# A linear-attention gate product stacked for one pass, and its chunk-end decays issued one step earlier

## The chip, the cores and the metric

The kernel runs on one core of a Trainium2 chip. The metric is the device time of one execution in microseconds (us), as the median of several runs. TensorE (PE in the profile, PEld for its weight loads) multiplies, VectorE (DVE), ScalarE (ACT) and GpSimd (POOL) do the elementwise work, and SyncE (SP) issues most DMAs.

## The reference, cut to what matters

Two layers of a streaming encoder over 512 tokens of width 1024. Each layer has a token mixer with three groups of heads (retention, stick-breaking attention, gated linear attention) and a convolutional feed-forward part. The change lies in the gated linear attention. `glr` is a projection of rank 16 and `b_i` the running sum of the log decays within a chunk of 64 tokens:

```
log_alpha = log_sigmoid(glr @ gla_w2 + gla_b) / 16        # (512 x 16) @ (16 x 256)
bcum  = cumsum(log_alpha within a chunk)
blast = bcum at the chunk's end
kv    = einsum(k * exp(blast - bcum), v)                  # decays to the chunk's end
inter = (q * exp(bcum)) @ state                           # decays from the chunk's start
state = exp(blast) * state + kv
w     = exp(-|b_t - b_s|)                                 # inside a chunk, either direction
intra = (q k w summed over d) @ v
```

All of it is in f32 and has to hold f32 accuracy.

## The kernel before, in words

Large products take three passes each: both operands are split into a rounded part (`hi`, type fp32r) and the rest (`lo`), and `mm3` sums hi·hi, hi·lo and lo·hi. For weights, `unit` loads 512 KB into `raw` (L360), ACT casts it to `hi` (L361) and DVE subtracts to get `lo` (L362). Activations `hnh`, `hnl` are split once. A projection `proj_T` is 24 matmuls of 128x512 into one PSUM bank named `pj`; everything else goes into banks named `ps`.

A mixer runs four kinds of work as generators, and a string of letters (`TOK`) sets in which turn they are advanced: `p` one projection, `g` a step of linear attention, `s` a step of stick-breaking or retention, `f` four loads of the modulation weights (`ada`, 256 KB each), which DVE multiplies and sums (L255) while the mixer runs. `ada` tiles have three buffers, `raw` two. A scheduling layer then puts every engine's instructions into one fixed order, by its own estimates; at run time an engine executes that order strictly, so an instruction that waits holds all behind it on its engine.

`gla_pair` (L653) handles two heads. It makes the gate (a product with K of 16 in plain f32: `w2` 16x256 and `glrT` 16x512, tiles filled at L569 to L574), the running sum `b` by a scan (L665), and then seven score steps `n` = 0 to 6. Step `n` issues 16 small score products, then, for `n` < 6, the decays of the next level (`decays`, L669 to L679), then merges the scores under a mask (L701). Behind the last step (`n` = 6) stand `kd` (L706, exponential on ACT at L226, L709), `qd` (an exponential and L711) and `dl`. The next step of the generator transposes `kd` on PE (L95), copies the result (L722) and multiplies it with the values; DVE rolls the states forward (L740, L742), and the output products follow.

There are two such pairs in each layer, so four gate products and four `kd` chains in the program. Each gate product issues from the two lines

```
with seq("g"):
    PE.matmul(ps, res["w2"][:, j * P : j * P + P], res["glrT"], start=True, stop=True)
```

Of the kernel before, what the change touches and what calls it, by code (L numbers as in the profile page):

```python
# [12 lines left out]
F32R = mybir.dt.float32r  # L13
# [3 lines left out]
ALU = mybir.AluOpType  # L17
AX = mybir.AxisListType

P = 128  # L20
S = 512
# [40 lines left out]
LEVELS = (64, 32, 16, 8, 4, 2)  # L62
# [36 lines left out]
def trunk(ctx: ExitStack, tc: tile.TileContext, A, out, dbg=None):  # L99
# [18 lines left out]
    def nm(s):  # L118
        cnt[0] += 1
        return f"{s}_{cnt[0]}"  # L120

    def T(tag="m", shape=(P, 512), dt=F32):
        tag = TMAP.get(tag, tag)
        return tiles[tag].tile(list(shape), dt, tag=tag, name=nm(tag + "_"))

    def small(n):
        return sp.tile([P, 8], F32, tag="s", name=nm("s"))[:, :n]

    def bank(t):
        t = PMAP[t]  # L130
        return banks[t].tile([P, 512], F32, tag=t, name=nm(t))
# [4 lines left out]
    def psz():  # L136
        return bank("pz")
# [4 lines left out]
    def psg():  # L142
        return bank("pg")

    V, SC, G, PE = nc.vector, nc.scalar, nc.gpsimd, Recorder(nc.tensor)

    @contextmanager
    def seq(kind):

        mode = MODE[kind]  # L150
        m = (None, PE.last, PE.lastp)[mode]
        if m is not None:
            with tc.issue_after(m.ins):
                yield
        else:
            yield
        if kind == "p":
            PE.lastp = PE.last
# [4 lines left out]
    def ld(t, src, gated=False, kind=None):  # L163
        q = QUEUE.get(kind, "sp")
        if q != "sp":
            return (G if q == "g" else SC).dma_start(t, src)


        m = lastw[0] if gated else start["ld"]
        if m is None:  # L170
            r = nc.sync.dma_start(t, src)
        else:
            with tc.issue_after(m.ins):
                r = nc.sync.dma_start(t, src)
        if start["on"]:
            start["ld"] = r
        return r
# [5 lines left out]
    def as32(t):  # L183
        return t.bitcast(F32)
# [39 lines left out]
    def act(*a, **k):  # L224
        with tc.issue_after(tables[0].ins):
            last_act[0] = SC.activation(*a, **k)  # L226
# [316 lines left out]
    def mixer(l, hnh, hnl, after):  # L543
# [3 lines left out]
        res = {}  # L547
# [16 lines left out]
        def use_gv(tb, ps):  # L564
            vtok[tb] = T("gv", (P, 272))
            SC.copy(vtok[tb], ps[:, 0:272])
            if tb == NTB - 1:
                w2 = T("gl", (16, 256))
                ld(w2, A["gla_w2"][l], True)  # L569
                ps = psg()  # L570
                for t in range(NTB):
                    PE.transpose(ps[0:16, t * P : t * P + P], vtok[t][:, 256:272], ident)
                glrT = T("gl", (16, S))
                SC.copy(glrT, ps[0:16, :])  # L574
                res["w2"], res["glrT"] = w2, glrT

        trig, dms = [], {}

# [14 lines left out]
        def project(n):  # L593
            if n[:2] in ("sv", "gv", "rv"):
                src, w, use = {"sv": (A["wsv"], 384, use_sv), "gv": (A["wgv"], 272, use_gv),
                               "rv": (A["wrv"], 384, use_rv)}[n]
                if n in start:
                    for tb, ps in enumerate(start.pop(n)):
                        use(tb, ps)
                else:  # L600
                    yield from proj_tok(src[l], w, hnh, hnl, use)
                res[n] = True
                return
            res[n] = project_T(n[:2], int(n[2]))
            yield
# [47 lines left out]
        def gla_pair(j):  # L653
            gq, gk, _ = need(f"gq{j}", f"gk{j}", "gv")
            ps = psg()
# [13 lines left out]
            def decays(m):  # L669
                E = T("ge")  # L670
                bv = b.rearrange("p (n h t) -> p n h t", h=2, t=m // 2)
                Ev = E.rearrange("p (n h t) -> p n h t", h=2, t=m // 2)
                r = bv[:, :, 0, m // 2 - 1 : m // 2].to_broadcast([P, S // m, m // 2])
                V.tensor_tensor(Ev[:, :, 0, :], r, bv[:, :, 0, :], ALU.subtract)
                V.tensor_tensor(Ev[:, :, 1, :], bv[:, :, 1, :], r, ALU.subtract)
                act(E, E, AF.Exp, scale=-1.0 / TAU)
                kt, qt = T("ge"), T("ge")
                V.tensor_tensor(kt, gk, E, ALU.mult)
                V.tensor_tensor(qt, gq, E, ALU.mult)  # L679
                return kt, qt  # L680
# [3 lines left out]
            for n in range(len(LEVELS) + 1):  # L684
                kt, qt = cur

                ps = [psg(), (psz, pso, psg)[GB]()]
                with seq("g"):
                    for c in range(NCH):
                        odd, cs = 64 * (c % 2), slice(c * CH, c * CH + CH)  # L690
                        for h in range(2):
                            PE.matmul(ps[h][odd : odd + 64, c // 2 * CH : c // 2 * CH + CH], kt[64 * h : 64 * h + 64, cs],
                                      qt[64 * h : 64 * h + 64, cs], start=True, stop=True)
                if n < len(LEVELS):
                    cur = decays(LEVELS[n])
                for h in range(2):
                    p3 = ps[h][:, 0 : S // 2].rearrange("p (c t) -> p c t", t=CH)
                    if n == 0:
                        SC.copy(sc[:, h], p3)
                    else:  # L700
                        V.copy_predicated(sc[:, h],  # L701
                                          C["lev"][:, n - 1, :].unsqueeze(1).to_broadcast([P, NCH // 2, CH]), p3)
                if n == len(LEVELS):
                    b3 = b.rearrange("p (c t) -> p c t", t=CH)
                    kd, qd = T("gl"), T("gl")
                    V.tensor_tensor(kd.rearrange("p (c t) -> p c t", t=CH),  # L706
                                    b3[:, :, CH - 1 : CH].to_broadcast([P, NCH, CH]), b3, ALU.subtract)
                    act(kd, kd, AF.Exp, scale=-1.0 / TAU)
                    V.tensor_tensor(kd, kd, gk, ALU.mult)  # L709
                    act(qd, b, AF.Exp, scale=-1.0 / TAU)  # L710
                    V.tensor_tensor(qd, qd, gq, ALU.mult)  # L711
                    dl = small(NCH)
                    act(dl, b3[:, :, CH - 1], AF.Exp, scale=-1.0 / TAU)
                yield
            tap(f"gs{l}{j}", sc.rearrange("p h c t -> p (h c t)"))

            ps = psg()
# [100 lines left out]
        def ret_pair(j):  # L818
# [12 lines left out]
            with seq("r"):  # L831
# [4 lines left out]
            yield from normed(ro[j], pvl[:, PV["rn"] + j : PV["rn"] + j + 1])  # L836

        chains = {"g": chain(*(gla_pair(j) for j in range(2))),
                  "s": chain(*((sb_pair if x[0] == "s" else ret_pair)(int(x[1])) for x in SORD.split()))}
        alive = set(chains)  # L840
# [50 lines left out]
        for tb in range(NTB):  # L891
            cs = slice(tb * P, tb * P + P)
            ps = psz()
# [79 lines left out]
    if WARM:  # L973

        ps = psz()
# [196 lines left out]
```

## Time and profile before

| | us |
|---|---|
| median of 3 runs | 1393.89 |
| the runs | 1394.96, 1389.60, 1393.89 |
| the profiled execution | 1389.99 |
| its span, first to last instruction | 1388.2 |
| PE busy | 1352.6 (97%) |
| DVE busy | 837.9 (60%) |
| ACT busy | 633.9 (46%) |

The two mixers lie at about 15 to 345 us and 700 to 1015 us of the span, the feed-forward parts behind each. A busy PE is not a PE at its peak, since its matmuls overlap and their ends are modelled: the distance from one matmul's start to the next says more than its duration. "Idle before" is the time an engine had nothing running, with the instruction that ended the wait. An engine's granted clock of 1.00 is 2.4 GHz and 0.50 is 1.2 GHz.

### The profile page before, as it was taken

Reading aid. Unit: us, or ns where it says so; the run is one execution under the profiler, and the core shown is the slowest. Engines: PE = TensorE matmul, PEld = TensorE weight load, DVE = VectorE, ACT = ScalarE, POOL = GpSimd, SP = SyncE. Lnnn points to the kernel's source line nnn. Section 1 sums busy time; section 2 is a strip of 40 time slices with the busy share of each in tenths; the row PEclk is TensorE's granted clock in tenths of the full one; section 3 lists DMA queues with packets and bytes.
Section 4 is the critical chain, followed back from the end, with each engine's and each line's share of the span. In section 5 each row is a group of like instructions: output and inputs, shape, how many; then the busy total and the mean of one; then the engine's idle time right before and its main releaser. Section 6 shows DMA issues by size and latency. Waiting matters only on the chain.

```text
span 1388.2 us, 19780 instructions
## 1 busy us (share of the span) xinstructions
PE 1352.6 (97%) x7619; PEld 1109.0 (80%) x7619; DVE 837.9 (60%) x1572; ACT 633.9 (46%) x1033; POOL 66.5 (5%) x121
## 2 busy tenths in 40 slices
PE   8999999999999999999999999999999999999997
PEld 5887667767988878888899877777898888888886
DVE  4559997666888864524563587777575444443232
ACT  5456465755533333322254556665564333332220
POOL 1000000001000000000030000000110000000000
PEclk9999999999999999999999999999999999999999
DMA  9635461215677852233753222111433222222233
GB/s 323 223 120 168 157 220 50 77 33 178 229 251 253 265 184 95 91 106 116 245 172 123 69 92 76 39 69 61 146 128 121 91 96 102 91 102 96 91 106 106
DMA packets 72463, 186.23 MB, mean 134 GB/s; under 512 B 8832, under 2 KB 9904, under 8 KB 72368
## 3 DMA queue, kind: packets, MB, share of 16 engines
q1 hardware_dynamic: 69056, 176.39, 37.6%
q0 software_dynamic: 3008, 8.41, 1.7%
q8 instruction: 60, 0.98, 0.3%
q14 instruction: 35, 0.29, 0.1%
q10 hardware_dynamic: 304, 0.16, 0.0%
HBM read 176.51 MB, written 8.41 MB: 133 GB/s over the span
## 4 chain that ended last, share of the span: by engine, by line
PE 63%; DVE 16%; DMA 9%; issue 6%; ACT 4%; POOL 1%; SPq 0%; DVEq 0%; POOLq 0%; ACTq 0%
PE pj L92 36%; PE ps L92 27%; DMA ada<-ada 8%; DVE lo L362 3%; DVE ada L255 3%; ACT hi L361 1%; DMA raw<-wsv 0%; POOL s L295 0%; DMA m__117_557<-ada 0%; DMA raw<-wu 0%; ACT junk L307 0%; DVE m__180_958 L701 0%; DMA raw<-wT 0%; DMA m__6_119<-x 0%; DVE hnl L342 0%
## 5 line engine op out<-in xcount | busy, mean ns | idle before, releaser
L362 DVE TENSOR_TENSOR lo<-raw,hi 128x1024 fp32r<-128x1024 f32 (+2 forms) x208 | 245.8, 1183 | 260.0 <-ACT hi L361 251.6
L92 PE MATMUL pj<-hnh,hi 128*128 128x512 f32 x976 | 384.0, 393 | 0.8 <-DVE mod1sc L260 0.8
L92 PE MATMUL pj<-hnh,lo 128*128 128x512 f32 x976 | 382.3, 392 | 2.2 <-DVE lo L362 2.2
L92 PE MATMUL pj<-hnl,hi 128*128 128x512 f32 x976 | 382.1, 392 | 0.0
L361 ACT CAST hi<-raw 128x1024 fp32r<-128x1024 f32 (+2 forms) x208 | 211.4, 1018 | 334.0 <-PE pj L92 174.5
L92 PEld LDWEIGHTS pj<-hnh,lo 128*128 128x128 f32 x976 | 183.7, 188 | 40.6 <-DVE lo L362 2.5
L92 PEld LDWEIGHTS pj<-hnh,hi 128*128 128x128 f32 x976 | 183.7, 188 | 40.7 <-issue 3.6
L92 PEld LDWEIGHTS pj<-hnl,hi 128*128 128x128 f32 x976 | 183.8, 188 | 37.5 <-issue 0.8
L255 DVE SCALAR_TENSOR_TENSOR ada<-ada,cB 128x512 f32<-128x512 f32 x160 | 106.7, 686 | 32.2 <-DMA ada<-ada 31.8
L295 POOL TENSOR_TENSOR s<-s,nhalf 128x1 f32<-128x1 f32 x32 | 19.3, 604 | 728.0 <-DVE s L293 720.1
L92 PE MATMUL pj<-hi,hnh 128*128 128x384 f32 (+1 forms) x160 | 51.2, 320 | 0.0
L92 PE MATMUL pj<-hi,hnl 128*128 128x384 f32 (+1 forms) x160 | 51.0, 319 | 0.0
L92 PE MATMUL pj<-lo,hnh 128*128 128x384 f32 (+1 forms) x160 | 51.0, 319 | 0.0
L92 PE MATMUL ps<-hnh,hi 128*128 128x256 f32 x128 | 36.6, 287 | 2.6 <-ACT hnh L341 2.6
L92 PE MATMUL ps<-hnl,hi 128*128 128x256 f32 x128 | 36.6, 286 | 1.2 <-DVE hnl L342 1.2
L92 PE MATMUL ps<-hnh,lo 128*128 128x256 f32 x128 | 36.1, 283 | 0.0
L524 ACT ACTIVATE junk<-ps 128x512 bf16<-128x512 f32 x16 | 9.5, 595 | 52.7 <-PE ps L92 52.7
L92 PEld LDWEIGHTS pj<-hi,hnh 128*128 128x128 f32 x160 | 30.1, 188 | 0.4
L92 PEld LDWEIGHTS pj<-lo,hnh 128*128 128x128 f32 x160 | 30.1, 188 | 0.3
L92 PEld LDWEIGHTS pj<-hi,hnl 128*128 128x128 f32 x160 | 30.1, 188 | 0.0
L92 PEld LDWEIGHTS ps<-hnh,hi 128*128 128x128 f32 x128 | 24.4, 192 | 3.5 <-ACT hnh L341 3.5
L92 PEld LDWEIGHTS ps<-hnl,hi 128*128 128x128 f32 x128 | 24.5, 191 | 1.9 <-DVE hnl L342 1.9
(2810 smaller groups left out, 2497.7 us busy)
## 6 DMA issues: line engine op xcount, KB each, us to landing
raw<-wu SPq DMA_DIRECT2D x88, 512.0 KB, 3.3
ada<-ada SPq DMA_DIRECT2D x160, 256.0 KB, 3.4
raw<-wd SPq DMA_DIRECT2D x44, 512.0 KB, 3.2
raw<-wT SPq DMA_DIRECT2D x42, 512.0 KB, 3.6
raw<-wo SPq DMA_DIRECT2D x16, 512.0 KB, 3.3
raw<-wsv SPq DMA_DIRECT2D x8, 384.0 KB, 3.8
raw<-wrv SPq DMA_DIRECT2D x8, 384.0 KB, 3.0
raw<-wgv SPq DMA_DIRECT2D x8, 272.0 KB, 2.9
```

The source lines that it names most:

```text
L92: self.last = self.e.matmul(*a, **k)
L255: V.scalar_tensor_tensor(raw, raw, 1.0, cB[h], ALU.mult, ALU.mult, accum_out=pt[:, 4 * h + j : 4 * h + j + 1])
L295: G.tensor_tensor(r, v, nhalf, ALU.pow)
L361: SC.copy(h, raw)
L362: V.tensor_tensor(l_, raw, as32(h), ALU.subtract)
L524: SC.activation(junk, ps, AF.Square, accum_out=ss)
```

## The change

First, the gate's operands. Instead of one f32 product with K of 16, both operands go into zeroed tiles of 128 rows in fp32r (`w3`, `g3`): rows 0 to 15 hold the rounded weights against the rounded activations, rows 32 to 47 the weights' rest against the rounded activations, rows 64 to 79 the rounded weights against the activations' rest. One fp32r product over K of 128 gives the sum of the three. Two memsets on POOL, three small operations on DVE for the weights, one on DVE for the activations and a second copy on ACT are new in each layer.

Second, `kd`, `qd` and `dl` are issued behind step `n` = 5 instead of `n` = 6, one step of the generator earlier.

```diff
             if tb == NTB - 1:
-                w2 = T("gl", (16, 256))
+
+                w2, w3, g3 = T("gl", (16, 256)), T("gl", (P, 256), F32R), T("gl", dt=F32R)
+                for t in (w3, g3):
+                    G.memset(as32(t), 0.0)
                 ld(w2, A["gla_w2"][l], True)
+                for r in (0, 64):
+                    V.tensor_copy(w3[r : r + 16, :], w2)
+                V.tensor_tensor(w3[32:48, :], w2, as32(w3[0:16, :]), ALU.subtract)
                 ps = psg()
                 for t in range(NTB):
                     PE.transpose(ps[0:16, t * P : t * P + P], vtok[t][:, 256:272], ident)
-                glrT = T("gl", (16, S))
-                SC.copy(glrT, ps[0:16, :])
-                res["w2"], res["glrT"] = w2, glrT
+                for r in (0, 32):
+                    SC.copy(g3[r : r + 16, :], ps[0:16, :])
+                V.tensor_tensor(g3[64:80, :], ps[0:16, :], as32(g3[0:16, :]), ALU.subtract)
+                res["w2"], res["glrT"] = w3, g3
...
-                if n == len(LEVELS):
+                if n == len(LEVELS) - 1:
                     b3 = b.rearrange("p (c t) -> p c t", t=CH)
                     kd, qd = T("gl"), T("gl")
```

The scheduling layer answers with another order. Lines of the changed kernel are 7 higher from here on (L706 becomes L713, L709 L716, L711 L718, L722 L729, L701 L708, L783 L790, L786 L793, L740 L747).

On DVE in layer 0, second pair, the operations of `kd` and `qd` stood behind the rotation of a retention key (L587 to L399, which follows the last stick-breaking block, L786). Before:

```order
L786 TENSOR_TENSOR m__549_2783<-m__547_2777,m__548_2782 128x512
L587 STREAM_SHUFFLE m__557_2822<-pj_2792 128x512
L588 TENSOR_TENSOR m__556_2821<-pj_2792,m__133_709 128x512
L589 TENSOR_TENSOR m__557_2822<-m__557_2822,m__134_710 128x512
L590 TENSOR_TENSOR m__556_2821<-m__556_2821,m__557_2822 128x512
L399 SCALAR_TENSOR_TENSOR m__560_2829<-m__556_2821,m__558_2827 64x512
L399 SCALAR_TENSOR_TENSOR m__561_2830<-m__556_2821,m__559_2828 64x512
L706 TENSOR_TENSOR m__569_2892<-m__449_2287 128x512
L711 TENSOR_TENSOR m__570_2893<-m__570_2893,m__424_2176 128x512
L709 TENSOR_TENSOR m__569_2892<-m__569_2892,m__377_1929 128x512
```

In the changed kernel they stand ahead of the three stick-breaking blocks of that head (L790, L793):

```order
L686 TENSOR_TENSOR m__538_2747<-m__425_2184,m__536_2742 128x512
L713 TENSOR_TENSOR m__539_2752<-m__450_2295 128x512
L718 TENSOR_TENSOR m__540_2753<-m__540_2753,m__425_2184 128x512
L716 TENSOR_TENSOR m__539_2752<-m__539_2752,m__378_1937 128x512
L362 TENSOR_TENSOR lo_3213<-raw_3210,hi_3212 128x1024
L790 SCALAR_TENSOR_TENSOR m__545_2776<-ps_2763,m__545_2776 128x256
L793 TENSOR_TENSOR m__547_2782<-m__545_2776,m__546_2781 128x256
```

So the three operations moved past two `lo`, three blocks of stick-breaking and the whole rotation; the transposes on PE (L95) moved ahead of 18 matmuls of the last projection.

On ACT at the same place, the exponentials of `qd` and `kd` (L226 from m__449 and m__569) and a cast of `hi` stood between the copies of the key's halves (L398) and the copy of the transposed `kd` (L722). Before:

```order
L398 ACTIVATE m__558_2827<-m__556_2821 64x512 x2
L398 ACTIVATE m__559_2828<-m__556_2821 64x512 x2
L627 COPY m__566_2870<-pj_2845 128x512
L226 ACTIVATE m__570_2893<-m__449_2287 128x512
L226 ACTIVATE m__569_2892<-m__569_2892 128x512
L361 CAST hi_3280<-raw_3278 128x1024
L722 COPY m__573_2929<-ps_2924 128x512
```

In the changed kernel the copy (L729) follows the projection's copy at once:

```order
L398 ACTIVATE m__562_2844<-m__560_2838 64x512 x2
L398 ACTIVATE m__563_2845<-m__560_2838 64x512 x2
L634 COPY m__570_2887<-pj_2862 128x512
L729 COPY m__574_2937<-ps_2932 128x512
L634 COPY m__581_2974<-pj_2949 128x512
L361 CAST hi_3288<-raw_3286 128x1024
```

Both exponentials have gone from this stretch to the one ahead of it.

On DVE in layer 0, first pair, modulation rows (L255) stand between two `lo` of weights. Before, from the first `lo` to the second:

```order
L362 TENSOR_TENSOR lo_1901<-raw_1898,hi_1900 128x1024
L587 STREAM_SHUFFLE m__348_1792<-pj_1762 128x512
L588 TENSOR_TENSOR m__347_1791<-pj_1762,m__133_709 128x512
L589 TENSOR_TENSOR m__348_1792<-m__348_1792,m__134_710 128x512
L255 SCALAR_TENSOR_TENSOR ada_1931,s_1809<-ada_1931,cB_109 128x512
L590 TENSOR_TENSOR m__347_1791<-m__347_1791,m__348_1792 128x512
L255 SCALAR_TENSOR_TENSOR ada_1934,s_1809<-ada_1934,cB_110 128x512
L255 SCALAR_TENSOR_TENSOR ada_1937,s_1809<-ada_1937,cB_109 128x512
L399 SCALAR_TENSOR_TENSOR m__351_1799<-m__347_1791,m__349_1797 64x512
L399 SCALAR_TENSOR_TENSOR m__352_1800<-m__347_1791,m__350_1798 64x512
L362 TENSOR_TENSOR lo_2013<-raw_2010,hi_2012 128x1024
```

In the changed kernel:

```order
L362 TENSOR_TENSOR lo_1909<-raw_1906,hi_1908 128x1024
L594 STREAM_SHUFFLE m__349_1800<-pj_1770 128x512
L595 TENSOR_TENSOR m__348_1799<-pj_1770,m__133_709 128x512
L596 TENSOR_TENSOR m__349_1800<-m__349_1800,m__134_710 128x512
L255 SCALAR_TENSOR_TENSOR ada_1827,s_1817<-ada_1827,cB_110 128x512
L597 TENSOR_TENSOR m__348_1799<-m__348_1799,m__349_1800 128x512
L255 SCALAR_TENSOR_TENSOR ada_1939,s_1817<-ada_1939,cB_109 128x512
L255 SCALAR_TENSOR_TENSOR ada_1942,s_1817<-ada_1942,cB_110 128x512
L399 SCALAR_TENSOR_TENSOR m__352_1807<-m__348_1799,m__350_1805 64x512
L399 SCALAR_TENSOR_TENSOR m__353_1808<-m__348_1799,m__351_1806 64x512
L255 SCALAR_TENSOR_TENSOR ada_1945,s_1817<-ada_1945,cB_109 128x512
L362 TENSOR_TENSOR lo_2021<-raw_2018,hi_2020 128x1024
```

One row more stands ahead of the second `lo`, and the last of the four is now the one directly before it. On SP the load of that last row has moved behind a load of 512 KB (`raw`).

## Rows read from the trace of the kernel before

**Rows 1.** Page, part 1: busy time of each engine.
```profile
PE 1352.6 (97%) x7619; PEld 1109.0 (80%) x7619; DVE 837.9 (60%) x1572; ACT 633.9 (46%) x1033; POOL 66.5 (5%) x121
```
**Rows 2.** Windows: stretch, length, busy us (instructions) by engine, granted clock, DMA share, GB/s.
```profile
100.00:200.00 100.00, 94.42 (x666) 73.69 (x665) 92.84 (x228) 56.82 (x96) 7.01 (x14) 0.98 0.55 179
200.00:300.00 100.00, 93.39 (x679) 69.17 (x680) 72.99 (x137) 60.52 (x103) 3.38 (x5) 0.98 0.20 70
...
500.00:600.00 100.00, 100.00 (x442) 82.81 (x442) 49.70 (x58) 39.77 (x50) 0.00 (x0) 1.00 0.29 103
```
**Rows 3.** Tile view of layer 0's `glrT`: durations ns min/median/max, starts, form.
```profile
L92 PE MATMUL ps<-m__163_870,m__161_863 x4: 587/640/692, 84.3 to 213.0; 16*128 16x512 f32 x4
L574 ACT COPY m__163_870<-ps x1: 575/575/575, 73.7 to 73.7; 16x512 f32<-16x512 f32 x1
```
**Rows 4.** PE in time, first gate product of layer 0: start, us, what.
```profile
83.98 0.39 PE L92 MATMUL pj<-hnh,lo 128*128 128x512 f32 x1
84.30 1.12 PE L92 MATMUL ps<-m__163_870,m__161_863 16*128 16x512 f32 x2
85.35 0.50 PE L92 MATMUL pj<-hnh,hi 128*128 128x512 f32 x1
85.68 0.40 PE L92 MATMUL pj<-hnl,hi 128*128 128x512 f32 x1
```
**Rows 5.** PE in time, second gate products of layers 0 and 1.
```profile
212.47 1.12 PE L92 MATMUL ps<-m__163_870,m__161_863 16*128 16x512 f32 x2
213.52 0.50 PE L92 MATMUL ps<-m__349_1797,m__402_2047 128*128 128x512 f32 x1
...
879.54 1.12 PE L92 MATMUL ps<-m__1310_6989,m__1308_6982 16*128 16x512 f32 x2
880.59 0.64 PE L92 MATMUL ps<-m__1485_7879,m__1254_6629 128*64 128x512 f32 x1
```
**Rows 6.** PE in time, layer 0, second pair: [idle before, released by].
```profile
277.37 0.39 PE L92 MATMUL pj<-hnh,lo 128*128 128x512 f32 x1
279.62 0.63 PE L95 MATMUL ps<-ident,m__569_2892 128*128 128x128 f32 x4 [1.86 <-DVE m__569_2892 L709]
280.93 0.49 PE L92 MATMUL ps<-m__154_780,m__573_2929 64*128 64x128 f32 x4 [0.68 <-ACT m__573_2929 L722]
```
**Rows 7.** ACT, then DVE, in time there.
```profile
274.46 1.29 ACT L398 ACTIVATE m__558_2827<-m__556_2821 64x512 fp32r<-64x512 f32 x2 [0.44 <-DVE m__556_2821 L590]
276.95 0.56 ACT L627 COPY m__566_2870<-pj 128x512 f32<-128x512 f32 x1
280.29 0.59 ACT L722 COPY m__573_2929<-ps 128x512 f32<-128x512 f32 x1 [0.68 <-PE ps L95]
...
278.79 0.68 DVE L709 TENSOR_TENSOR m__569_2892<-m__569_2892,m__377_1929 128x512 f32<-128x512 f32 x1
```
**Rows 8.** Windows of 2 us with a low granted clock.
```profile
170.00:172.00 2.00, 2.00 (x6) 1.63 (x5) 1.97 (x6) 0.75 (x2) 0.00 (x0) 0.50 0.90 342
...
282.00:284.00 2.00, 2.00 (x8) 0.72 (x7) 1.28 (x5) 0.00 (x0) 0.00 (x0) 0.50 0.69 246
```
**Rows 9.** PE and DVE in time, layer 0, first pair.
```profile
168.67 0.64 PE L92 MATMUL pj<-hnh,lo 128*128 128x512 f32 x1 [2.21 <-DVE lo L362]
169.10 0.63 PE L92 MATMUL pj<-hnh,hi 128*128 128x512 f32 x1
...
165.38 0.69 DVE L255 SCALAR_TENSOR_TENSOR ada<-ada,cB 128x512 f32<-128x512 f32 x1 [1.59 <-DMA ada<-ada]
167.39 1.22 DVE L362 TENSOR_TENSOR lo<-raw,hi 128x1024 fp32r<-128x1024 f32 x1
```
**Rows 10.** PE in time, layer 1, second pair.
```profile
954.91 0.63 PE L95 MATMUL ps<-ident,m__1667_8892 128*128 128x128 f32 x4 [0.41 <-DVE m__1667_8892 L709]
```
**Rows 11.** DVE in time behind the gate operands of layer 0.
```profile
77.06 0.96 DVE L362 TENSOR_TENSOR lo<-raw,hi 128x768 fp32r<-128x768 f32 x1 [2.85 <-ACT hi L361]
```
**Rows 12.** DMA issues: KB each, median us to landing.
```profile
raw<-wT SPq DMA_DIRECT2D x42, 512.0 KB, 3.6
```

## Prediction

> **What bounds the kernel now.** I read the page's busy times first, then the windows of 100 us, then PE's own time line at the places that the change touches, and last what ended PE's waits there. The page has PE busy for 97% of the span and DVE for 60% [rows 1]. In the feed-forward part PE runs without a gap: 442 matmuls in 100 us, 0.226 us from start to start, at full clock [rows 2]. That is the pace of a 128x512 fp32r matmul when nothing waits, and the reader should measure all else against it. In the mixers PE misses about 6% of its time, and DVE is at 93% in the first half of layer 0's mixer and at 73% in the second [rows 2]. So what counts is how many PE slots a step takes, and how long PE stands at the few places where DVE, ACT or a DMA is late. The feed-forward parts are not touched.
>
> **The gate products.** There are four in the program, two in each layer, and each is two records, x4 in a layer [rows 3]. For the first of layer 0 the stretch from 83.98 to 85.68 holds one projection matmul, the two records and another projection matmul: 1.70 us [rows 4]. One fp32r product leaves three slots of 0.226, that is 0.68; saved: 1.02. The first of layer 1 stands in the same surroundings, so another 1.02 (estimate). The second of layer 0 follows an f32 product: it takes 1.05 from 212.47 to 213.52 [rows 5]; a single slot with the joint that shows behind the f32 product in layer 0 (85.35 to 85.68, 0.33 [rows 4]) leaves 0.33, and the next product loses its joint of 0.11. Saved: 0.83. The second of layer 1 lies between two f32 products, 879.54 to 880.59 [rows 5], and keeps one joint: 1.05 less 0.33, or 0.72. Sum: 3.6 us. An fp32r product with K of 128 in a stream of such products is exactly what the projections are, so I see no reason for a longer slot; the bounds are nothing saved (if the product took as long as f32) and four times 1.05, or 4.2.
>
> The two records start 1.05 us apart from what follows, which is 4.6 slots of 0.226 [rows 2, 5]. The Trainium skill, page "FP8 and Floating Point Precision", section "TensorE Precision Notes", says that true FP32 takes four passes through the array. By that rule alone each product would save three slots, 2.7 us over the four; the trace shows the rest as joints around the f32 product, and I go by the trace.
>
> Do these slots lie on the path? PE runs through at both first products. What DVE does behind them begins with results of PE, so it begins earlier too. I count them whole.
>
> **The new operations of the gate.** In each layer: on ACT a second copy of 16x512, 0.58 like the one shown [rows 3]; on DVE two copies and a subtraction of 16x256 and one subtraction of 16x512, at most 0.68 each by the 128x512 operation shown [rows 7], 2.7 in all; two memsets on POOL, which is busy for 5% [rows 1]. DVE has stood idle for 2.85 us when the next `lo` begins at 77.06 [rows 11], and the gate product follows only at 84.30 [rows 4]. The DMA of `w2` now stands behind one load of 384 KB on SP, and DVE's copies wait for it; behind them wait two `lo` and a query's halves, for weights that are read after 85 us. I take 0. If the cover were gone, 3.3 per layer, or 6.6 at most; below nothing I see no gain.
>
> **The chunk-end decays, layer 0, second pair.** PE ends its projection at 277.37 plus a slot, 277.60, waits until 279.62 for L709, transposes, and waits again for the copy L722; the first product with it starts at 280.93 [rows 6]. In the new order the transposes stand 18 projection matmuls earlier. Then PE's own work up to that product ends at 277.60 plus the transposes' four slots (0.45, estimate by a quarter of 0.226 per 128 columns, doubled for f32), 278.05. The copy on ACT now follows the projection's copy directly: 276.95 + 0.56 + 0.59 = 278.10 instead of 280.88 [rows 7]. The product could start at 278.15, 2.8 us sooner. Against it: three DVE operations of 0.68, 2.0 us in sum [rows 7], and two exponentials now stand ahead of the stick-breaking blocks, whose end releases the rotation and so the copies L398 [rows 7]. DVE idles for a quarter of this stretch [rows 2], so part of it is absorbed; I take 0.8 late, and a gain of 2.0. Bounds: 0.8 (all late) and 2.8.
>
> Behind that wait the granted clock is 0.50, so 1.2 GHz, in the window of 282 to 284 [rows 8]. If PE no longer stands still there, up to 1.2 us more comes back (estimate: the stretch holds some 3 us at half pace, less the state updates on DVE that would then be late next). I take 0, since the copy may still be a little late.
>
> The Trainium skill, page "TensorE: Matmul & The Clock Gate", section "The HAM clock gate", says that idleness lowers the array's clock and sustained work restores it; the trace agrees, at half pace behind both long waits. By it, the sum would have the 1.2 as well.
>
> **The same, elsewhere.** In layer 1, second pair, PE waits 0.41 for L709 [rows 10]; the subtraction now comes sooner, so 0.4 goes. First pairs: PE waits for the transposes little or not at all; 0.
>
> **What is moved with it: layer 0, first pair.** PE waits 2.21 us for a `lo` at 168.67 and then runs at 0.43 per matmul [rows 9]. That `lo` starts at 167.39, behind modulation rows whose DMA was late by 1.59 us [rows 9]. In the new order one row more stands before it, and the last one's load comes behind 512 KB on SP. But those loads compete anyway, the rotation's halves that stood between are now done earlier, and DVE reaches the first `lo` sooner by one row. I take 0, with bounds of 3.8 to the good (2.2 and eight slots at 0.43 instead of 0.23) and 3.6 to the bad, a load of 512 KB [rows 12].
>
> **Sum.** 3.6 + 2.0 + 0.4 = 6.0 us less. The profiled execution has 1389.99, the span 1388.2 with 1.8 around it; against it the sum gives 1384.0. That execution is one of the fast ones: the median of the runs is 1393.89, 3.9 higher. The mean of the four executions known is 1392.1, and from it I forecast 1386.
>
> **Rivals.**
> *Eaten in layer 0.* DVE is at 93% between 100 and 200 us [rows 2]. If it is the bound there, PE only arrives sooner at the wait of 168.67 [rows 9], and what was won before is given back; likewise the second pair wins only its lower bound. Left: the second gate of layer 0 (0.8), layer 1's 1.7, 0.8 and 0.4, 3.7 less: 1388. For it: that wait exists. Against: DVE's queue starts with PE's results.
> *More than counted.* The wait of 168.67 goes and the clock stays up: 3.8 and 1.2 more, 11.0 in sum: 1381. For it: both stand behind late work that the order now changes. Against: nothing makes the DMAs faster.
> *Slower.* One mechanism: `lo` behind modulation rows in DVE's strict order, rows that wait for loads behind 512 KB on SP. It costs 3.6 [rows 12] plus 1.6 of low clock each time, 5.2. Once, it eats the gain; from the third time on the kernel is slower by 5.2 x 3 - 6 = 9.6: 1402. For it: raw loads moved ahead of rows at several places. Against: a raw load that comes sooner also makes its own `lo` sooner.
> *The gate saves nothing.* If fp32r with K of 128 took as long as f32, 2.4 would remain: 1390.
>
> **How the numbers follow.** The measurement tells about 0.5% from no change, 7 us; faster than that means below 1386.9. The forecast's case, 5 to 7 less, has 0.60 and straddles this line, 0.35 faster and 0.25 same. More than counted: 0.13, faster. Eaten in layer 0: 0.14, same. The gate saves nothing: 0.03, same. Slower: 0.10, of it 0.09 beyond the bound and 0.01 same. So faster 0.48, same 0.43, slower 0.09. The range leaves out the slower case and the extreme of the good one: 1380 to 1393.5.
>
> **What would show it.** PE's distance from the projection matmul before the first gate to the second matmul behind it: 0.7 instead of 1.70 us. No wait for the subtraction of `kd` (now L716) in either second pair, the first product with the copy 2 us sooner relative to the projection, and perhaps full clock behind it. At the `lo` of the first pair, the wait between 1 and 4 us. The forecast is wrong if PE's waits in layer 0 grow by more than the gates save, or if the new rows on DVE delay the `lo` of the retention values.

## The result, and the profile after

The changed kernel takes 1382.89 us (median of 7 runs, 1382.18 to 1387.69) against 1389.86 for the kernel before beside it (7 runs, 1388.45 to 1394.96). The medians differ by 7.0 us. The ratio of the runs is 0.9946, 95% interval 0.993 to 0.9962, which is 7.5 us faster, 5.3 to 9.7. The profiled execution has 1385.05 us, its span 1383.3. It started badly: at the last projection before the first gate PE stands 2.15 us later than in the profile of before, long ahead of anything that the change touches. The same program profiled again (a run below) stands 0.21 later there. So places are compared between neighbours, not by the clock on the wall.

The page of the kernel after, part 1, as in [rows 1]:

```profile
PE 1348.7 (97%) x7615; PEld 1108.3 (80%) x7615; DVE 841.1 (61%) x1580; ACT 635.1 (46%) x1035; POOL 68.1 (5%) x125
```

Windows of the kernel after, with the columns of [rows 2] (the granted clock is the third number from the end):

```profile
100.00:200.00 100.00, 95.08 (x677) 73.80 (x676) 94.68 (x232) 57.34 (x98) 7.02 (x14) 1.00 0.56 179
200.00:300.00 100.00, 94.73 (x694) 71.95 (x693) 75.34 (x142) 65.30 (x111) 3.46 (x5) 1.00 0.21 70
500.00:600.00 100.00, 100.00 (x443) 82.81 (x442) 46.62 (x55) 36.96 (x46) 0.00 (x0) 1.00 0.31 105
...
170.00:172.00 2.00, 2.00 (x11) 1.45 (x11) 1.83 (x5) 1.94 (x6) 0.00 (x0) 1.00 0.82 249
282.00:284.00 2.00, 1.59 (x8) 1.25 (x9) 1.81 (x7) 0.30 (x1) 0.00 (x0) 1.00 0.11 43
```

Both windows of layer 0 that had 0.50 [rows 8] have full clock in this execution (so that part of what its trace shows against before is clock, see below), and DVE is fuller in the first half of the mixer than it was: 94.68 against 92.84 [rows 2].

PE in time in the kernel after: the gates, then the first pair of layer 0, its second pair, the second pair of layer 1, and the first product of layer 0's feed-forward part:

```profile
86.13 0.39 PE L92 MATMUL pj<-hnh,lo 128*128 128x512 f32 x1
86.35 0.39 PE L92 MATMUL ps<-m__163_865,m__162_864 128*128 128x512 f32 x1
86.58 0.39 PE L92 MATMUL pj<-hnh,hi 128*128 128x512 f32 x1
86.81 0.39 PE L92 MATMUL pj<-hnl,hi 128*128 128x512 f32 x1
...
168.22 0.50 PE L92 MATMUL pj<-hnh,hi 128*128 128x512 f32 x1
168.56 0.40 PE L92 MATMUL pj<-hnl,hi 128*128 128x512 f32 x1
169.02 0.50 PE L92 MATMUL pj<-hnh,hi 128*128 128x512 f32 x1
169.35 0.40 PE L92 MATMUL pj<-hnl,hi 128*128 128x512 f32 x1
169.59 0.40 PE L92 MATMUL pj<-hnh,lo 128*128 128x512 f32 x1
...
274.48 0.39 PE L92 MATMUL pj<-hnh,lo 128*128 128x512 f32 x1
276.92 0.49 PE L92 MATMUL ps<-m__154_780,m__574_2937 64*128 64x128 f32 x4 [2.05 <-ACT m__574_2937 L729]
...
340.32 0.39 PE L92 MATMUL ps<-hnh,hi 128*128 128x256 f32 x1 [1.13 <-ACT hnh L341]
...
950.01 0.66 PE L95 MATMUL ps<-ident,m__1657_8799 128*128 128x128 f32 x4
```

Read against the groups of before: the first gate now takes 0.68 from 86.13 to 86.81 where it took 1.70 [rows 4]. At 169.59 the product with `lo` starts without a wait, where there were 2.21 us [rows 9]; ahead of it now stand two pairs of `hi` products, the second pair (169.02, 169.35) from the next projection. The transposes of both second pairs no longer wait ([rows 6, 10] had 1.86 and 0.41), but in layer 0 PE still waits 2.05 for the copy.

ACT, then DVE, in time in the kernel after: the copy (L729, formerly L722) and what stands before it, the new gate operations, and the `lo` of the first pair:

```profile
274.64 1.28 ACT L398 ACTIVATE m__563_2845<-m__560_2838 64x512 fp32r<-64x512 f32 x2
275.82 0.56 ACT L634 COPY m__570_2887<-pj 128x512 f32<-128x512 f32 x1
276.29 0.58 ACT L729 COPY m__574_2937<-ps 128x512 f32<-128x512 f32 x1
...
78.53 0.60 DVE L574 CAST m__162_864<-m__161_863 16x256 fp32r<-16x256 f32 x2 [0.68 <-DMA m__161_863<-gla_w]
79.61 0.96 DVE L362 TENSOR_TENSOR lo<-raw,hi 128x768 fp32r<-128x768 f32 x1
...
168.11 1.22 DVE L362 TENSOR_TENSOR lo<-raw,hi 128x1024 fp32r<-128x1024 f32 x1
```

The `lo` behind the gate's operands comes at 79.61, 2.55 later than at 77.06 [rows 11]; 2.15 of it is the late start. The idle time of 2.85 has taken the new operations up.

### The profile page after: what moved, and what is told of

It is laid out like the page before. It is cut to its first block, busy times and chain, and to the rows that moved or that the text cites. A ratio compares the mean times of both kernels' runs of the same rounds, so it can differ in the third digit from the quotient of the medians.

```text
span 1383.3 us, 19798 instructions
## 1 busy us (share of the span) xinstructions
PE 1348.7 (97%) x7615; PEld 1108.3 (80%) x7615; DVE 841.1 (61%) x1580; ACT 635.1 (46%) x1035; POOL 68.1 (5%) x125
## 4 chain that ended last, share of the span: by engine, by line
PE 60%; DVE 17%; DMA 11%; issue 6%; ACT 5%; POOL 1%; SPq 0%; DVEq 0%; POOLq 0%; ACTq 0%
PE pj L92 35%; PE ps L92 25%; DMA ada<-ada 7%; DVE lo L362 3%; DVE ada L255 3%; ACT hi L361 1%; DMA raw<-wT 1%; DMA m__52_259<-ada 0%; DMA m__1231_6545<-x 0%; POOL s L295 0%; DMA m__71_333<-ada 0%; DMA m__117_557<-ada 0%; DMA m__83_386<-ada 0%; DMA raw<-wu 0%; ACT junk L307 0%
## 5 line engine op out<-in xcount | busy, mean ns | idle before, releaser
L255 DVE SCALAR_TENSOR_TENSOR ada<-ada,cB 128x512 f32<-128x512 f32 x160 | 106.9, 686 | 33.9 <-DMA ada<-ada 33.7
```

Source lines behind the costliest of these rows:

```text
L255: V.scalar_tensor_tensor(raw, raw, 1.0, cB[h], ALU.mult, ALU.mult, accum_out=pt[:, 4 * h + j : 4 * h + j + 1])
```

## The experiments

Each run was compared with the kernel before on the same chip. The second column holds that comparison (the ratio and its interval times the median of before there). Three columns are shifts read from the traces: the start of one and the same PE instruction in both profiles, as the change in its distance between two points. "Layer 0" runs from the last projection before the first gate (83.98 in before) to the first product of the feed-forward part (345.15), "FF" from there to layer 1's first gate (769), "layer 1" from there to the end of the score steps (952). Minus is faster. The column "clock" says how much more or less of layer 0's stretch half clock takes than in before: 1 minus the granted clock, summed over the stretch. In before that is 3.4 us, at two places, 168 to 173 and 281 to 285.

| kernel | us against before, 95% | layer 0 | clock | FF | layer 1 |
|---|---|---|---|---|---|
| changed, first profile | -7.5 (-9.7 to -5.3) | -6.98 | -3.4 | +1.22 | -0.81 |
| changed, again | -6.8 (-9.3 to -4.3) | -5.03 | +1.7 | -0.64 | -1.26 |
| gate alone | -1.1 (-3.1 to +0.8) | -1.52 | -1.7 | +0.71 | -1.25 |
| decays alone | -5.2 (-7.2 to -3.1) | -4.82 | -1.7 | +0.33 | -0.15 |
| decays, first pairs | -2.6 (-4.6 to -0.7) | -2.21 | -1.7 | +0.11 | -0.27 |
| decays, second pairs | 0.0 (-2.2 to +2.4) | -0.63 | -1.7 | +2.15 | +0.79 |
| decay matrices on POOL | +1.3 (-1.0 to +3.6) | -3.32 | -1.7 | +1.62 | +0.32 |
| float32 gate four times | +10.9 (+7.7 to +13.9) | +2.95 | +1.7 | -1.02 | +8.23 |
| changed, early steps | -10.6 (-13.4 to -7.7) | -10.27 | -3.4 | -0.61 | -0.39 |
| before, early steps | -3.6 (-5.8 to -1.4) | -6.10 | 0.0 | -0.87 | -0.22 |
| changed, layer 1's gate only | -5.2 (-7.4 to -2.9) | -5.36 | -3.4 | -0.93 | -1.21 |

The feed-forward part is the same work in all of them and scatters over 3 us, so one profile's shift is good to a microsecond or so at best, and in layer 0 only between profiles that lost alike to the clock. The two profiles of the changed kernel show how much that matters: one program in one order, -6.98 and -5.03. The timed runs average over it. The mean granted clock of a whole execution is 0.996 both for the changed kernel (run again) and for before beside it; the difference, 0.0005, is 0.7 us of some 1390.

### The gate alone

```diff
-                if n == len(LEVELS) - 1:
+                if n == len(LEVELS):
```

(in the changed kernel)

> Only the stacked gate product; the decays to a chunk's end stay in the step after the last level. Theory A (each part gives what its own place shows): -3.3 us (-2.7 to -4.2) against the kernel before; about 0.7 us round each of the four gate products in place of 1.5 to 1.7; the wait for `lo` in the first pair of layer 0 stays near 2.2 us with the cold matmuls behind it, since VectorE's order there is that of before; the transposes of layer 0's second pair still wait 1.5 to 2 us. Theory B (nearly all of the 7 us is the order that the decays' move changes, and the shorter gate is used up by the next wait): 0 to -1.5 us.

Measured: -1.1 us (-3.1 to +0.8), in theory B's range; of theory A's range the interval holds only the weak end. PE in time in this kernel, the `lo` of the first pair and the transposes of layer 0's second pair:

```profile
167.97 0.50 PE L92 MATMUL pj<-hnh,lo 128*128 128x512 f32 x1 [0.90 <-DVE lo L362]
...
279.24 0.63 PE L95 MATMUL ps<-ident,m__570_2900 128*128 128x128 f32 x4 [2.74 <-DVE m__570_2900 L716]
```

The wait for `lo` is still there, at 0.90 and not near 2.2 as theory A had it, and the wait for the subtraction of `kd` has grown from 1.86 [rows 6] to 2.74: PE comes sooner and DVE does not. In layer 0's stretch PE's idle time grows from 13.9 to 15.0. Layer 1 keeps 1.25 in this profile, up to 952. This profile also has a stretch at half clock behind layer 1's scores that before has not, worth 1.6 us:

```profile
962.00:964.00 2.00, 2.00 (x7) 0.92 (x8) 1.09 (x3) 0.97 (x2) 0.00 (x0) 0.50 0.00 0
```

Such a stretch stands behind those scores in two more of the profiles (decays alone; layer 1's gate only) and not in the rest; what decides it stays open.

### The decays alone, and each pair alone

```diff
-                if n == len(LEVELS):
+                if n == len(LEVELS) - 1:            # both pairs
+                if n == len(LEVELS) - (j == 0):     # first pairs
+                if n == len(LEVELS) - (j == 1):     # second pairs
```

(in the kernel before; one of the three)

> Only the decays one step earlier, in both pairs; the gate is the float32 product of before. Theory A: -4 us (-2.5 to -5.5): some 2.4 from the second pairs, the rest from the wait for `lo` in the first pair of layer 0, which falls below 0.5 us. Theory B: -5.5 to -7 us, the whole of the change. If the named parts alone counted as in the prediction's sum (order of the first pair worth nothing): -2.4 us.

> The decays one step earlier in the first pair of each layer alone; second pairs and gate as before. Here no wait of the transposes of 0.3 us or more goes, only the order of VectorE round the first pair of layer 0 moves. Theory A, with the order counted: -2 us (-1 to -3.8), the wait for `lo` at about 168 us below 0.5 us and the matmuls behind it at full clock. Theory C (the moved order is worth nothing in the end, as the prediction's sum took it: the wait comes back later): -0.5 to +0.5 us.

> The decays one step earlier in the second pair of each layer alone; first pairs and gate as before. The prediction's sum: -2.4 us (-0.8 to -3.2), -2.0 of it in layer 0 (wait of 1.86 us for the last subtraction gone, the first product with the copy about 2 us sooner) and -0.4 in layer 1. Theory C: -4 to -5 us, since under it the first pairs give nothing and the whole of the decays' gain is here. Theory B (it is the first pair's order): 0 to -1 us.

Both pairs: -5.2 us (-7.2 to -3.1), in theory A's range, with theory B's not excluded. First pairs: -2.6 (-4.6 to -0.7), theory A. Second pairs: 0.0 (-2.2 to +2.4), theory B; the -2.4 of the prediction's sum lies just outside the interval. PE, then DVE, in time with the first pairs moved:

```profile
166.80 0.50 PE L92 MATMUL pj<-hnh,hi 128*128 128x512 f32 x1
167.14 0.40 PE L92 MATMUL pj<-hnl,hi 128*128 128x512 f32 x1
167.61 0.50 PE L92 MATMUL pj<-hnh,hi 128*128 128x512 f32 x1
167.94 0.40 PE L92 MATMUL pj<-hnl,hi 128*128 128x512 f32 x1
168.18 0.39 PE L92 MATMUL pj<-hnh,lo 128*128 128x512 f32 x1
...
166.63 1.22 DVE L362 TENSOR_TENSOR lo<-raw,hi 128x1024 fp32r<-128x1024 f32 x1
```

DVE begins that `lo` at 166.63, 0.76 sooner than in before (167.39, [rows 9]), so DVE accounts for the smaller part of a wait of 2.21. The larger part is PE's: it is ready for the product at 168.18, where in before it was at 166.46, the end of the wait less its length. Of these 1.7 us, 0.6 are two `hi` products of the next projection that now stand ahead of the one that needs `lo` (167.61 and 167.94); the rest PE is late by already ahead of them. With the gate alone DVE begins as early, at 166.69, PE's order is that of before, and 0.90 of the wait is left. Of the kernels here that keep PE's order of before, four have the wait: 0.90 (gate alone), 1.59 (second pairs), 1.53 (gate four times) and 0.58 (before, early steps). The six profiles in which the first pair is moved have none. At the end of layer 0 the trace shows -2.21 and the time -2.6. How much of the trace's is the wait is open, for the half clock of 170 to 172 [rows 8], up to 1.7 us of before's profile, did not return behind any of the four waits and so is not part of every execution.

With the second pairs moved, the same places as in [rows 6]:

```profile
272.68 0.62 PE L95 MATMUL ps<-ident,m__538_2744 128*128 128x128 f32 x4
280.88 0.49 PE L92 MATMUL ps<-m__154_780,m__573_2929 64*128 64x128 f32 x4 [1.84 <-ACT m__573_2929 L722]
```

Two waits of 1.86 and 0.68 have become one of 1.84 for the copy. It gains 1.1 between 250 us and the end of layer 0's mixer, and layer 1's transposes gain 0.45. The time does not show it. First and second pairs alone add up to -2.6 and both together give -5.2; with intervals of some 2 us on each, whether the two help each other is not settled.

### The decay matrices on another queue

```diff
-QUEUE = {"row": "g", "small": "a", "out": "g"}
+QUEUE = {"row": "g", "small": "a", "out": "g", "dm": "g"}
```

(in the kernel before)

> The kernel before, with retention's two decay matrices (256 KB each) loaded over GpSimd's queue in place of SyncE's; gate and chunk-end decays as before. It asks why `lo` is late at 168.67 us in the first pair of layer 0. Theory A (the modulation rows that stand ahead of that `lo` on VectorE wait for loads that SyncE issues behind the two decay matrices): their waits of 0.45 and 1.59 us fall to under 0.5 in sum, the wait for `lo` to under 1 us, the matmuls behind it keep full clock, and the time falls by 1.5 us (0 to -2.5). Rival (those loads are late because the DMA engines are full, whatever the queue): the waits stay within 0.5 us of what they were, and the time too.

Measured: +1.3 us (-1.0 to +3.6). DVE's waits for modulation rows, then PE, in this kernel:

```profile
166.33 0.69 DVE L255 SCALAR_TENSOR_TENSOR ada<-ada,cB 128x512 f32<-128x512 f32 x1 [0.20 <-DMA ada<-ada]
168.63 0.69 DVE L255 SCALAR_TENSOR_TENSOR ada<-ada,cB 128x512 f32<-128x512 f32 x1 [0.27 <-DMA ada<-ada]
...
169.89 0.50 PE L92 MATMUL pj<-hnh,hi 128*128 128x512 f32 x1 [0.55 <-ACT hi L361]
```

The rows wait 0.47 together, as the theory had it, but the time did not fall. And the run cannot say what the shorter waits are worth: it also put two products of the next projection ahead of the late one on PE, just as the moved decays do. Inconclusive.

### The float32 gate four times over

```diff
+                for _ in range(4):
                     PE.matmul(ps, res["w2"][:, j * P : j * P + P], res["glrT"], start=True, stop=True)
```

(in the kernel before)

> The kernel before, with each of the four float32 gate products issued four times over into the same bank: twelve more. It prices the gate's time on TensorE at each place. Theory A (the slots lie on the path everywhere, as the prediction counted them): +2.7 to +3.2 us at each place and +11 to +12.6 us in all. Theory D (layer 0's mixer has slack behind the gates, since VectorE and ScalarE are late there anyway, which is why the gate alone gave little): layer 0 pays less than half of its 6 us by its end, layer 1 nearly all of its 6, and +7 to +9 us in all.

Measured: +10.9 us (+7.7 to +13.9), between the ranges of the two theories. By the traces layer 0 pays 2.95 and layer 1 8.23. PE in time at the first gate:

```profile
84.07 3.69 PE L92 MATMUL ps<-m__163_870,m__161_863 16*128 16x512 f32 x8
87.70 0.50 PE L92 MATMUL pj<-hnh,hi 128*128 128x512 f32 x1
...
90.11 0.63 PE L92 MATMUL pj<-hnl,hi 128*128 128x512 f32 x1
90.54 0.63 PE L92 MATMUL pj<-hnh,lo 128*128 128x512 f32 x1
```

Four products take 3.63, 0.907 each with the joints at both ends, which is 4.0 slots of 0.227; in the middle one starts 0.86 behind the other, 3.8 slots. The 1.05 that one took alone [rows 5] thus holds 0.14 to 0.19 of joints. The Trainium skill, page "FP8 and Floating Point Precision", section "TensorE Precision Notes", gives four passes for true FP32; the trace agrees, at 3.8 to 4.0 slots. Each place cost more than three products, though: the projection behind them runs at half pace, 0.43 from 90.11 to 90.54. The windows of the same kernel:

```profile
84.00:88.00 4.00, 4.00 (x10) 1.70 (x10) 0.96 (x1) 1.62 (x3) 0.00 (x0) 1.00 0.71 217
88.00:90.00 2.00, 2.00 (x7) 1.59 (x6) 0.75 (x1) 1.84 (x3) 0.00 (x0) 0.65 0.24 90
90.00:92.00 2.00, 2.00 (x6) 1.54 (x6) 0.65 (x1) 0.00 (x0) 1.27 (x1) 0.50 0.00 0
```

Low clock stands behind the other three places too (218 to 226, 774 to 782, 890 to 895). So layer 0 makes PE 6.7 us busier, 5.4 for six products and the rest clock, and its idle time falls by 3.8, from 13.9 to 10.1: 2.95 are left to pay. Layer 1 up to 952 makes it 9.5 busier, its idle time falls by 1.3, and 8.2 are left. So theory D's picture holds by place: waits that PE has in layer 0 anyway take up more than half of what is added there, and little of it in layer 1. The sum lies above theory D's range, with low clock in it that no expectation had.

### The changed kernel again

The edit is none.

> The changed kernel once more, beside the same runs of the kernel before as its neighbours here: -7 us (-5 to -9). If the two halves simply add, it is -1.1 and -5.1 from the runs of each half alone: -6.2 us.

Measured: -6.8 us (-9.3 to -4.3); the two halves add up to -6.3. PE's waits in layer 0 in this profile, two of them new, and the first product of the feed-forward part:

```profile
106.64 0.50 PE L92 MATMUL ps<-m__199_1043,tri 128*128 128x512 f32 x1 [0.67 <-DVE m__199_1043 L793]
...
141.92 0.69 PE L92 MATMUL ps<-m__285_1514,m__284_1513 64*64 64x64 f32 x32 [0.70 <-DVE m__285_1514 L686]
...
276.41 0.49 PE L92 MATMUL ps<-m__154_780,m__574_2937 64*128 64x128 f32 x4 [2.06 <-ACT m__574_2937 L729]
...
340.33 0.39 PE L92 MATMUL ps<-hnh,hi 128*128 128x256 f32 x1 [1.14 <-ACT hnh L341]
```

In before the first of these waits was 0.27 and the second none. The wait for the copy is that of the first profile, but a window of this one, 2 us behind it, has half clock, and so has a stretch from 178 to 184. Two windows of this profile, then the first profile's window behind the same wait:

```profile
182.00:184.00 2.00, 2.00 (x7) 1.71 (x7) 2.00 (x4) 0.85 (x2) 0.00 (x0) 0.50 0.85 253
278.00:280.00 2.00, 2.00 (x7) 0.66 (x8) 1.90 (x5) 0.00 (x0) 0.00 (x0) 0.50 0.00 0
...
278.00:280.00 2.00, 2.00 (x15) 0.93 (x16) 1.52 (x3) 0.41 (x1) 0.00 (x0) 1.00 0.00 0
```

This profile stood 1.94 us ahead of the first one before the first gate, and both reach the feed-forward part at the same time, 340.33 and 340.32. The lead does not all go into waits: 0.70 of it is gone by 178.69, and the same instructions then take 5.86 us at half clock (178.69 to 184.55) where the first profile takes 3.56 (179.93 to 183.49).

### Layer 1's gate only

```diff
+                if l:      # layer 0 keeps w2, glrT and the float32 product
```

(in the changed kernel, round the new tiles and operations of the gate)

> The changed kernel, with the float32 gate of before in layer 0 and the stacked gate in layer 1 alone. Theory D (layer 0's mixer has slack behind its gates): by the end of layer 0's mixer at most 1 us behind the changed kernel, and the whole 0 to +1 us against it, near -6.3 us against the kernel before. Theory A (the gate's slots in layer 0 are paid in full): +1.85 us by the end of layer 0's mixer and in the whole, near -5 us against the kernel before.

Measured: -5.2 us (-7.4 to -2.9), near theory A's -5; its median, 1385.40, is 0.9 above the changed kernel's 1384.51, where theory D had 0 to 1. The time does not decide. Nor do the traces. This profile wins 5.36 in layer 0, 0.33 more than the changed kernel's second profile, which lost 5.1 to half clock where this one lost nothing; and 1.6 less than its first, which lost nothing either. Between those two at full clock, PE is 1.95 busier here, which is the two gates, and its idle time is only 0.33 less. That speaks for theory A, though the first profile also came 2.4 us later to the first gate. The instruction at which the changed kernel waits 0.70 for DVE (second profile) comes at this time here, with no wait:

```profile
141.66 0.69 PE L92 MATMUL ps<-m__284_1506,m__283_1505 64*64 64x64 f32 x32
```

From the projection ahead of the first gate it stands 57.93 away here, 57.73 and 57.42 in the two profiles of the changed kernel: of the 1.02 saved at that gate 0.2 and 0.5 are left there. So the first gate's saving is in large part taken back by waits within 60 us; what both gates are worth at the end of the mixer, between nothing and 1.6 of 2.0, stays open.

### Two steps earlier, with and without the change

The profile after leaves 2.05 us at the copy, with ACT idle for 2.08 (up to 272.11) while it was ready. In layer 0's string of `TOK`, letters 74 to 82, two `g` (last scores; transposes and copy) move ahead of two projections:

```diff
-gsppgsgpg
+gsggppsgp
```

> The changed kernel, with linear attention's next two steps (last scores; transposes and copy) in the second pair of layer 0 issued ahead of two projections, so that ScalarE has the copy before the last exponential and the rotation's halves. In the changed kernel TensorE still waits 2.05 us for that copy at 276.92. Theory A (the copy is late only by its place on ScalarE): that wait goes, the first product with the copy stands between projection matmuls, and the time falls by a further 2 us against the changed kernel (-1 to -3), some 9 us against the kernel before. Rival (the state updates or the rotation's halves are late next and take the wait over): within 0.7 us of the changed kernel.

> The kernel before, with linear attention's last scores and its transposes and copy in layer 0's second pair issued ahead of two projections, as in the run before, but with the float32 gate and the decays behind the last level. It asks whether the place of the copy on ScalarE alone, without the change, gives what the second pair of layer 0 had to give. Theory A (it was the copy's place): the waits of 1.86 and 0.68 us at 277 to 281 go, and the time falls by 2 to 4 us against the kernel before. Rival (it takes the earlier decays: else the transposes wait for the subtraction of `kd`, only sooner): 0 to -1 us, with a wait for that subtraction of 1 us or more.

Measured: in the changed kernel -10.6 us (-13.4 to -7.7), median 1381.21 against 1384.51 for the changed kernel beside it; in the kernel before -3.6 (-5.8 to -1.4). ACT, then PE, in the first of the two:

```profile
269.31 0.58 ACT L729 COPY m__557_2828<-ps 128x512 f32<-128x512 f32 x1
...
271.37 0.49 PE L92 MATMUL ps<-m__154_780,m__557_2828 64*128 64x128 f32 x4
...
272.46 0.50 PE L92 MATMUL pj<-hnl,hi 128*128 128x512 f32 x1
```

The copy runs ahead of the last exponential and the rotation, its product stands among projection matmuls, and the wait is gone. Against the changed kernel it is 3.3 by the medians, a little more than theory A's 1 to 3, and 3.3 in layer 0 by the traces (-10.27 against -6.98, both at full clock from the same place on). This is the fastest of all kernels here. In the kernel before, the same move takes both waits of [rows 6] away without the earlier decays, as theory A had it, so they were not needed for that. It is worth about as much without the change (3.6, in theory A's range) as with it (3.3). As far as intervals of some 2 us can tell, the change had left most of what the copy's place has to give.

## Why the prediction was right, and by which steps

The time (1386 forecast, 1382.89 and 1384.51 measured; 6.0 us forecast, 7.5 and 6.8 measured) lies in the forecast's range. The sum was right while two of its terms were wrong in opposite directions; that it came out so near is luck.

**The gate products: right at the place, too large at the end.** Forecast 3.6 in four places. Between the same neighbours the traces show 1.02, 1.02, 1.03 and 0.83 in the changed kernel, 3.9 together. The step that failed is "I count them whole". The gate alone gives 1.1 in time (-0.8 to +3.1), and on top of the decays 1.6 to 2.3 (6.8 and 7.5 less 5.2). Layer 0 has waits that take back a part: DVE is busy for 95% from 100 to 200 us, PE finds at DVE's results (L793, L686) half or more of what it saved at the first gate, and six products more cost layer 0 2.95 where they cost layer 1 8.23. Layer 1 keeps about 1 of 1.86 by the traces up to 952: the five profiles with its stacked gate move by -0.4 to -1.3 there, the five without by -0.3 to +0.8, leaving the one with four products aside. The times do not show this division (layer 1's gate adds nothing to the decays alone, -5.2 both), but they cannot tell a microsecond. The rival "Eaten in layer 0" had this mechanism; I gave it 0.14, with the argument that DVE's queue starts with PE's results. That is true of single rows and not of an engine that is nearly full.

**The new operations at nothing: right.** With the gate alone PE is 0.86 behind before at 44 us, ahead of the new operations, and still 0.86 behind at the first gate; the idle time ahead of `lo` took them up.

**Layer 0, second pair: the mechanism right, the size not shown.** Forecast 2.0 (0.8 to 2.8). The wait for the subtraction is gone and the copy follows the projection's copy (275.82, 276.29), as the text had it. But the rotation's halves ahead of it make it later than the 0.8 allowed: relative to the projection, the product with the copy comes 1.1 sooner (2.44 behind it where it was 3.56), and not 2 us. From the scores at 250 us to the end of the mixer, the five profiles with this part of the change and the steps in their old places gain 1.1 to 2.2; but of three without it, two (gate alone, first pairs) gain nothing, and one (decay matrices on POOL), without half clock there, gains 1.8. In time the second pairs alone give 0.0 (-2.2 to +2.4), and on top of the first pairs 2.5.

**Layer 1, second pair: right.** Forecast 0.4; 0.45 in every kernel with the second pairs moved.

**The moved order in layer 0, first pair: the step that was sized wrong.** I took 0, because DVE's order gave the `lo` no better start, and named a wait of 1 to 4 us as the sign; there is none. DVE did begin it 0.76 sooner with the first pairs moved. Above all I followed only the engine that was waited for. On PE two products of the next projection had come to stand ahead of the late one, and three projection products had gone behind the transposes. It gives 2.6 (0.7 to 4.6) by the time and 2.2 by the trace, up to 1.7 of that clock. The gain of "More than counted" was there in part, without its argument about faster loads.

So by the times 1.3 to 2.5 us of gate that I had counted were not to be had, and some 2.6 of order that I had not counted were. The rivals "Slower" and "The gate saves nothing" have nothing for them: no matmul waits for a `lo` in the changed kernel, and the product takes one slot.

## What to carry to other kernels

A slot saved on the busiest engine may be taken back by waits where another engine is nearly full in the same stretch; lengthening the operation several times over shows layer by layer how much of its time is paid. Before two traces are compared, look at the granted clock of both: here half clock takes anything from 0 to 5.1 us of the same mixer. When a scheduler rewrites the order, read the new order of the engine that waits as well as of the one it waits for: a wait goes when other work moves ahead of it. And a wait that is left after a change names the next edit: moving two steps of issue was worth a further 3.3 us here.

## What was not expected of the hardware

TensorE's granted clock fell to 0.50 behind 3.6 us of float32 products with K of 16, though PE stood still at no point (100% busy in the windows from 84 to 92): 0.65 in 88 to 90, 0.50 in 90 to 92, and matmuls at 0.43. It fell behind the other three places too, with PE 100% busy ahead: 0.54 in 218 to 222, 0.58 in 774 to 778, 0.68 in 890 to 892. The Trainium skill, page "TensorE: Matmul & The Clock Gate", section "The HAM clock gate", ties the low level to an idle engine; this run shows it behind an engine that was never idle. Why it falls there stays open. Nor does a wait's length alone tell the clock behind it. The changed kernel waits 2.05 us for the copy in its first profile and 2.06 in its second; in 278 to 280, behind the wait, the clock is 1.00 in the one and 0.50 in the other (the lines of both stand above). So what the prediction set aside at 0, up to 1.2 us of clock at this place, comes in some executions and not in others.
